# A decoder block with dilated attention and an RG-LRU: a third output tile and swapped PSUM banks in the attention stage, other engines for a few small operations

## The chip, the cores and the metric

The kernel runs on one core of a Trainium2 chip. The metric is the time of one execution on the device in microseconds (us), as the median of several runs. One further execution was recorded by the hardware profiler; all rows of the profile come from it.

Five engines work side by side, each through its own instructions in order: TensorE (PE; its weight loads are PEld), VectorE (DVE), ScalarE (ACT), GpSimd (POOL) and SyncE (SP, which here issues most of the DMAs). They wait for one another by semaphores. PSUM, into which TensorE writes, has eight banks of 128 x 512 float32. SBUF holds all other tiles.

## The reference, cut to what matters

```python
proj = x @ w_in + b_in                       # x: (1, 2048, 1024), w_in: 1024 x 9216
q, k, v, g_attn, u_lru, g_lru, gate_logits = split(proj)
# 3 head groups of 8 heads (64 wide): (window, dilation) = (128,1), (512,4), (2048,16)
for g in range(3):                           # rotary q and k, keys gathered by stride
    o_g, lse_g = dilated_band_attention(q[g], k[g], v[g], window, dilation)
attn = sum(softmax(lses) * outs) * silu(g_attn);          y_a = attn @ w_attn_proj
h = rg_lru(causal_conv(u_lru));              y_b = (h * silu(g_lru)) @ w_lru_proj
merged = sigmoid(gate_a) * y_a + sigmoid(gate_b) * y_b
out = layer_norm(2 ** 0.25 * x + merged @ w_out + b_out) * ln_gain + ln_bias
```

Everything is float32. Within `dilated_band_attention` each block of 128 queries meets at most 256 keys: scores, maximum, exponential with its sum, and the weighted sum of values.

## The kernel before, in words

The order of the instructions on each engine is written out by hand. Work that is to come a step later is put on a list (`later(lag, fn)`) and emitted by `run(late)` at the start of that step. Each matmul of the reference is made of three, from a high and a low part of either operand. There are three stages, each with pools of its own, which lie one over the other in SBUF and PSUM: a tile of a later stage waits for what still uses the earlier one's memory.

**First stage: the projection** (`product`, L622), up to 1443.8 us of the profile. It works through 72 passes of seven or eight products of 12 matmuls each, in four PSUM banks (tag `q`). VectorE and ScalarE take the results out (`total`, L568 and L227), and chains of small operations (`qk_chain`, `lru`, `mg_chain` and others) finish them and store them to DRAM. Results lie in 32 slots of SBUF of 2 KB per partition, numbers 0 to 31; `take` gives out the slot that has been free for longest, but for results `y` of the last pass it prefers those in the list `LATE`. The last gates `y` go through a tanh on ScalarE (L384) and are stored by ScalarE's DMA queue (L386).

**Second stage: attention**, up to the first `yb` matmul at 1654.6 us. There are 12 units, one for each pair of heads (two heads of one group), in the order of dilation 1, 16, 4, 1, 16, 4 and so on. A unit has four steps, so there are `NG` = 48 steps `i` and three more to run out; one step has four blocks `j` of 128 queries, with the two heads `h`. Tiles and their operations, where L is the line in the profile:

- `scores(i)`: TensorE writes the scores into four tiles `s` (L1005), one bank each.
- `peak(i, j, h)`: VectorE adds the mask and takes the maximum into `sta` (L1012), a small tile for each unit, 3 buffers; `expo(i, j, h)`: ScalarE takes the exponential, with its sum also into `sta` (L1020).
- `turn(i, w)`: TensorE transposes the weights of two blocks (`w` = 0: blocks 0 and 1) into two tiles `pt` (L1030). These and `o` share the tag `t`, four banks.
- `bring(i, w, k, eng)`: the copy of one such tile from PSUM into `ptb`, by ScalarE (L1043) or VectorE (L1045).
- `values(i)`: TensorE multiplies with the values into `o` (L1058); `leave(i)`: VectorE copies `o` into the unit's output tile `ot` (L1067, L1071 and L1069 for dilations 1, 16 and 4), 128 x 2048 float32, 2 buffers.
- SP stores `ot` to `o_scr` (L1073 for each step, L1075 for a whole unit of dilation 16) and, once for each unit, `sta` to `st_scr` (L1080, L1082; four DMAs in L1085). It also loads the next units' keys (L816, tile `B`), queries (L826, tile `A`) and values (tile `V`); GpSimd and others split the keys into high and low part (L809, L811).

In one step the engines get their work in this order:

```python
light = copied and (unit((i - 2) // 4)[0] == 2 or i % 3 == 1)
scores(i); leave(i - 3)
bring(i - 2, 1, 1, dve)
if light: bring(i - 2, 1, 0, dve)
expo(i - 1, 2, 1)
if copied and not light: bring(i - 2, 1, 0, act)
expo(i - 1, 3, 0); expo(i - 1, 3, 1); peak(i, 0, 0); expo(i, 0, 0); # peaks of blocks 0 and 1
turn(i - 1, 0); bring(i - 1, 0, 0, act); bring(i - 1, 0, 1, dve)
# exponentials of blocks 0 and 1; peaks of block 2; values(i - 2); turn(i - 1, 1); peaks of block 3
```

`light` says which engine makes the copy `bring(i - 2, 1, 0)`: VectorE in the steps after a unit of dilation 16 and in each third step, ScalarE in the others. `unit(u)[0]` is the group, 2 for dilation 16.

A pool gives a tag its memory when the tag is first used. So in PSUM the scores `s` got the four banks that the projection's `q` had, and the tag `t` got those of its tags `t` and `g`. In the third stage `y` (four banks) came first, then `ct` (one) and `z` (three).

**Third stage**: the projection of the RG-LRU branch (`yb_job`, L1310 to L1316), the combination of the attention groups, the projection of attention (`ya_job`, L1388 to L1394, the sum `me` on GpSimd), and for each 128 rows `tt` the output matmul and the LayerNorm (`out_job`, `z` in L1420 to L1422). LayerNorm there: VectorE adds the residual (L1433), takes the statistics (L1436, L1439) into a small tile `mv` (mean, variance, two more columns); ScalarE takes the square root of the variance plus `EPS` (L1440); VectorE centres the first half of the columns (`centre`, L1444), inverts the root (L1448), improves it by one Newton step in four operations on one column (L1450 to L1453), scales the first half (L1457), centres the second and scales it. Each half is stored by a DMA. The last rows (`tt` = 15, `last`) take the same path, with SP's queue for the first half and ScalarE's for the second.

## Time and profile before

| | |
|---|---|
| time, median of three runs | 2114.82 us (2113.8 to 2116.68) |
| the profiled execution's time | 2113.77 us |
| its span in the profile | 2112.0 us |
| busy PE, DVE, ACT, POOL | 2088.6, 1663.8, 1120.5, 491.9 us |
| granted TensorE clock, mean | 0.997 |
| DMA | 524.69 MB, mean 248 GB/s |

A row of a timeline gives the start in us from the beginning of the span, the duration, the engine, the line of the kernel, the operation, out<-in by the tiles' names, the shapes, and how often it stands there in a run; in brackets is the idle time of the engine ahead of it and what ended it. A row of waits names who waited for whom: us in total, times, the longest. A row of a window gives the stretch, its length, each engine's busy time in it with its instructions, the granted clock of TensorE (1.00 is full), the busy share of the DMA engines and GB/s. A row of DMA issues gives how many, the size and the median us from issue to landing. A row of a group of instructions gives its busy time and the mean ns of one, then the idle time ahead of it.

### The profile page before, as it was taken

The numbers are of one execution on the slowest core, as the hardware profiler recorded it, in microseconds if no ns is written. First come the engines' busy times: TensorE is split into PE (matmuls) and PEld (weight loads), VectorE is DVE, ScalarE is ACT, GpSimd is POOL, SyncE is SP. The second block draws the span as 40 slices with busy tenths as digits, with TensorE's granted clock in tenths as the row PEclk, the third lists the DMA queues.
The fourth block names the chain that finished last, engine by engine and source line by source line (L and its number), as shares of the span: only waits on it lengthen the run. The fifth ranks groups of instructions, "written<-read, shape, count | busy, mean of one in ns | idle before, by whom it ended". The sixth has DMA issues, their size and how long they took to land.

```text
span 2112.0 us, 35853 instructions
## 1 busy us (share of the span) xinstructions
PE 2088.6 (99%) x12016; PEld 1729.0 (82%) x12016; DVE 1663.8 (79%) x3193; ACT 1120.5 (53%) x2348; POOL 491.9 (23%) x465
## 2 busy tenths in 40 slices
PE   8999999999999999999999999999999999999998
PEld 7888888888888888887888888888989888888887
DVE  8987888888888867787787887877989645576667
ACT  6356456457356565656567666667999411221100
POOL 1111111111111002231232232222536444331120
PEclk9999999999999999999999999999999999999999
DMA  8987997997997976677788788879998788864432
GB/s 271 268 273 223 276 284 209 284 289 234 273 291 237 329 221 200 213 238 212 249 252 274 255 251 269 257 223 382 296 303 263 238 283 274 302 245 155 161 110 70
DMA packets 345832, 524.69 MB, mean 248 GB/s; under 512 B 124208, under 2 KB 153904, under 8 KB 341808
## 3 DMA queue, kind: packets, MB, share of 16 engines
q1 hardware_dynamic: 325760, 489.54, 71.5%
q0 software_dynamic: 12256, 19.42, 5.5%
q10 hardware_dynamic: 7632, 13.44, 1.7%
q8 instruction: 96, 1.57, 0.3%
q14 instruction: 88, 0.72, 0.1%
HBM read 317.14 MB, written 190.45 MB: 240 GB/s over the span
## 4 chain that ended last, share of the span: by engine, by line
PE 91%; ACT 6%; DVE 2%; DMA 1%; issue 0%; SPq 0%
PE q L622 66%; ACT p L1020 5%; PE yb L1310 3%; PE yb L1311 3%; PE z L1420 3%; PE z L1421 3%; PE z L1422 3%; PE yb L1312 3%; PE ya L1388 1%; PE ya L1389 1%; PE ya L1390 1%; PE g L492 1%; PE vtp L358 1%; ACT ptb L1043 1%; PE o L1058 1%; DVE p L1012 1%
## 5 line engine op out<-in xcount | busy, mean ns | idle before, releaser
L622 PE MATMUL q<-xT,hS 128*128 128x512 f32 x1680 | 521.1, 391 | 0.0
L622 PE MATMUL q<-xT,l 128*128 128x512 f32 x1120 | 436.0, 389 | 0.0
L622 PE MATMUL q<-xB,hA 128*128 128x512 f32 x1248 | 389.1, 393 | 5.6 <-ACT xB L215 5.6
L622 PEld LDWEIGHTS q<-xT,hS 128*128 128x128 f32 x1680 | 312.8, 188 | 69.0 <-issue 5.5
L622 PE MATMUL q<-xB,l 128*128 128x512 f32 x904 | 353.0, 390 | 0.0
L622 PEld LDWEIGHTS q<-xB,hA 128*128 128x128 f32 x1248 | 233.7, 189 | 57.0 <-ACT xB L215 5.6
L622 PEld LDWEIGHTS q<-xT,l 128*128 128x128 f32 x1120 | 210.3, 188 | 44.1
L622 PEld LDWEIGHTS q<-xB,l 128*128 128x128 f32 x904 | 170.2, 188 | 36.3 <-DVE l L227 0.5
L1020 ACT ACTIVATE p<-p,sta 128x256 f32<-128x256 f32 (+1 forms) x384 | 175.7, 511 | 5.0 <-DVE sta L1012 4.8
L245 POOL DMA_DIRECT2D wS<-in_w_in_dram x70 | 62.0, 965 | 492.6 <-DMA wS<-in_w_in_dram 137.5
L622 PE MATMUL q<-xB,hS 128*128 128x512 f32 x560 | 174.0, 392 | 0.0
L622 PE MATMUL q<-xT,hA 128*128 128x512 f32 x560 | 173.0, 390 | 0.0
L269 ACT ACTIVATE hA<-wA 128x512 fp32r<-128x512 f32 x218 | 134.9, 623 | 55.4 <-DMA wA<-in_w_in_dram 19.8
L269 ACT ACTIVATE hS<-S 128x512 fp32r<-128x512 f32 x175 | 109.0, 623 | 76.4 <-DVE S L227 48.8
L227 POOL TENSOR_TENSOR S<-S,wA 128x512 f32<-128x512 f32 x35 | 45.6, 1304 | 392.3 <-DVE S L227 218.2
L622 PEld LDWEIGHTS q<-xT,hA 128*128 128x128 f32 x560 | 104.7, 188 | 23.0 <-issue 1.5
L622 PEld LDWEIGHTS q<-xB,hS 128*128 128x128 f32 x560 | 104.0, 188 | 22.4 <-issue 1.5
L1012 DVE CUSTOM_DVE_ANT_0 p<-s,mask 128x256 f32<-128x256 f32 (+1 forms) x384 | 116.7, 363 | 1.3 <-PE s L1005 0.9
L1421 PE MATMUL z<-wo,mh 128*128 128x512 f32 (+1 forms) x264 | 101.0, 383 | 0.0
L1422 PE MATMUL z<-wo,ml 128*128 128x512 f32 (+1 forms) x264 | 101.0, 383 | 0.0
L1420 PE MATMUL z<-wo,mh 128*128 128x512 f32 (+1 forms) x264 | 101.0, 383 | 0.0
L1310 PE MATMUL yb<-h,wl 128*128 128x512 f32 x256 | 100.2, 392 | 0.0
(201 smaller groups left out, 4262.9 us busy)
## 6 DMA issues: line engine op xcount, KB each, us to landing
wA<-in_w_in_dram SPq DMA_DIRECT2D x253, 256.0 KB, 4.8
wl_scr<-l SPq DMA_DIRECT2D x105, 512.0 KB, 5.2
l<-wl_scr SPq DMA_DIRECT2D x105, 512.0 KB, 4.8
sw<-y SPq DMA_DIRECT2D x384, 64.0 KB, 3.3
wS<-in_w_in_dram SPq DMA_DIRECT2D x70, 256.0 KB, 4.8
wS<-in_w_in_dram POOLq DMA_DIRECT2D x70, 256.0 KB, 6.4
qh_scr<-hi SPq DMA_DIRECT2D x48, 256.0 KB, 5.6
v_scr<-vs SPq DMA_DIRECT2D x48, 256.0 KB, 4.8
```

Source lines behind the costliest of these rows:

```text
L227: eng.tensor_tensor(out=out, in0=in0, in1=in1, op=op)
L245: pool.dma_start(t, w_part(s, x), accum_op=ALU.add)
L269: act.activation(h, r, AF.Copy)
L622: pe.matmul(bank, w[:, ks], x[:, kk, xx], start=(first and i == 0), stop=(last and i == 11))
L1012: dve.tensor_tensor_reduce(out=st["p", i, j][:, h, lo:256], in0=st["s", i, j // 2][h][:, j % 2, lo:256], in1=mask[:, lo:256], scale=1.0, s ...
L1020: act.activation(p, p, AF.Exp, scale=-1.0, bias=s[:, h:h + 1], accum_out=s[:, 2 + h:3 + h])
L1310: pe.matmul(yb, WL[f][:, 0, k], xx[:, 0], start=(k == 0), stop=False)
L1311: pe.matmul(yb, WL[f][:, 0, k], xx[:, 1], start=False, stop=False)
L1312: pe.matmul(yb, WL[f][:, 1, k], xx[:, 0], start=False, stop=(k == 7))
L1420: pe.matmul(z, mh[:, k], w[:, 0, hs], start=(k == 0), stop=False)
L1421: pe.matmul(z, mh[:, k], w[:, 1, hs], start=False, stop=False)
L1422: pe.matmul(z, ml[:, k], w[:, 0, hs], start=False, stop=(k == 7))
```

## The change

1. **`LATE`** lists seven slots, 7 to 13, where it had five, 31, 7, 8, 9 and 30.
2. **PSUM banks.** In attention the tag `t` is used first, by a tile that nothing else uses, so `t` gets the first four banks and `s` the last four. In the third stage `ct` and `z` come first, so `y` gets the last four.
3. **`ot`** has 3 buffers. That takes 8 KB more per partition, and the tiles that follow in SBUF (`ptb`, then some of keys, queries and values) lie 8 KB higher.
4. **Copies.** In steps 47 and 48 `bring(i - 1, 0, 0)` is VectorE's, and step 48 is `light`, so that its `bring(i - 2, 1, 0)` is VectorE's too.
5. **LayerNorm of the last rows.** GpSimd fills a column of `mv` with -0.5, adds `EPS` to the variance and raises the sum to the power of -0.5; VectorE centres both halves and then scales both. The square root, the inverse and the Newton step are left out there.
6. **LayerNorm of the other rows.** The Newton step takes three operations on one column instead of four.

```diff
-    LATE = [31, 7, 8, 9, 30]
+    LATE = [7, 8, 9, 10, 11, 12, 13]
...
     aps = stB.enter_context(tc.tile_pool(name="aps", bufs=2, space=PSUM, reuse_waits="tile"))
+    aps.tile([P, 4, P], F32, tag="t", name="t", bufs=4)
...
-            ot[u] = at_p.tile([P, S], F32, tag="ot", name=f"ot{u}")
+            ot[u] = at_p.tile([P, S], F32, tag="ot", name=f"ot{u}", bufs=3)
...
-        light = copied and (unit((i - 2) // 4)[0] == 2 or i % 3 == 1)
+        light = copied and (unit((i - 2) // 4)[0] == 2 or i % 3 == 1 or i == NG)
...
-            bring(i - 1, 0, 0, act)
+            bring(i - 1, 0, 0, act if i < NG - 1 else dve)
...
     fp = ctx.enter_context(tc.tile_pool(name="fp", bufs=2, space=PSUM, reuse_waits="tile"))
+    fp.tile([P, 4, P], F32, tag="ct", name="ct", bufs=1)
+    fp.tile([P, CH], F32, tag="z", name="z", bufs=3)
...
-        act.activation(mv[:, 2:3], mv[:, 1:2], AF.Sqrt, bias=epst)
         halves = (slice(0, CH), slice(CH, D))
 
         def centre(hs):
             dve.scalar_tensor_tensor(out=x[:, hs], in0=x[:, hs], scalar=mv[:, 0:1], in1=vec[1][:, hs],
                                      op0=ALU.subtract, op1=ALU.mult)
 
-        centre(halves[0])
-        dve.reciprocal(out=mv[:, 2:3], in_=mv[:, 2:3])
-
-        dve.tensor_scalar(out=mv[:, 1:2], in0=mv[:, 1:2], scalar1=EPS, scalar2=-0.5, op0=ALU.add, op1=ALU.mult)
-        dve.tensor_tensor(out=mv[:, 3:4], in0=mv[:, 2:3], in1=mv[:, 2:3], op=ALU.mult)
-        dve.tensor_scalar(out=mv[:, 3:4], in0=mv[:, 3:4], scalar1=mv[:, 1:2], scalar2=1.5, op0=ALU.mult, op1=ALU.add)
-        dve.tensor_tensor(out=mv[:, 2:3], in0=mv[:, 2:3], in1=mv[:, 3:4], op=ALU.mult)
+        if last:
+            pool.memset(mv[:, 3:4], -0.5)
+            pool.tensor_tensor(out=mv[:, 2:3], in0=mv[:, 1:2], in1=epst, op=ALU.add)
+            pool.tensor_tensor(out=mv[:, 2:3], in0=mv[:, 2:3], in1=mv[:, 3:4], op=ALU.pow)
+            for hs in halves:
+                centre(hs)
+        else:
+            act.activation(mv[:, 2:3], mv[:, 1:2], AF.Sqrt, bias=epst)
+            centre(halves[0])
+            dve.reciprocal(out=mv[:, 2:3], in_=mv[:, 2:3])
+
+            dve.tensor_scalar(out=mv[:, 1:2], in0=mv[:, 1:2], scalar1=EPS, scalar2=-0.5, op0=ALU.add, op1=ALU.mult)
+            dve.scalar_tensor_tensor(out=mv[:, 3:4], in0=mv[:, 2:3], scalar=mv[:, 2:3], in1=mv[:, 1:2], op0=ALU.mult, op1=ALU.mult)
+            dve.tensor_scalar(out=mv[:, 2:3], in0=mv[:, 3:4], scalar1=1.5, scalar2=mv[:, 2:3], op0=ALU.add, op1=ALU.mult)
         for hs, eng in zip(halves, (sp, act) if last else (act, act)):
-            if hs.start:
+            if hs.start and not last:
                 centre(hs)
             dve.scalar_tensor_tensor(out=x[:, hs], in0=x[:, hs], scalar=mv[:, 2:3], in1=vec[2][:, hs],
                                      op0=ALU.mult, op1=ALU.add)
```

## The prediction

> **What bounds the kernel now.** I read the page first, then the waits of TensorE, the windows of 6 us, and the timelines at the four places where the diff touches something.

> ```profile
> PE 2088.6 (99%) x12016; PEld 1729.0 (82%) x12016; DVE 1663.8 (79%) x3193; ACT 1120.5 (53%) x2348; POOL 491.9 (23%) x465
> ```

> TensorE is busy for 2088.6 of 2112.0 us, and the diff removes none of its work. What can be won lies in TensorE's gaps, in its clock, and behind its last matmul.

> ```profile
> PE q L622 <- ACT xB L215: 5.6, 1, 5.6
> PE pt L1030 <- DVE ot L1071: 3.4, 1, 3.4
> PE o L1058 <- ACT ptb L1043: 1.6, 6, 0.4
> PE pt L1030 <- ACT ptb L1043: 1.6, 4, 0.6
> PE pt L1030 <- DVE ot L1069: 1.1, 1, 1.1
> PE s L1005 <- DVE y L227: 0.5, 1, 0.5
> PE s L1005 <- DVE sta L1012: 0.5, 2, 0.3
> PE o L1058 <- DVE ptb L1045: 0.4, 1, 0.4
> ```

> The waits of TensorE, whole (us in total, times, longest). The 5.6 us lie at the start, which the diff leaves alone; all other rows are of attention, none of the third stage. The single ones are a stall within attention (3.4), one at its end (1.1, and 0.4) and one at its beginning (0.5), and each has a part of the change. The windows show that the 3.4 us are not the whole of it (columns: us, busy PE, PEld, DVE, ACT, POOL, granted clock, DMA share, GB/s):

> ```profile
> 1572.00:1578.00 6.00, 2.57 (x46) 2.36 (x44) 1.88 (x10) 2.31 (x13) 0.00 (x0) 0.97 0.75 118
> 1578.00:1584.00 6.00, 6.00 (x64) 5.55 (x62) 5.03 (x33) 5.06 (x25) 1.05 (x2) 0.50 1.04 416
> ```

> After the gap the granted clock is 0.50 for the whole of the next window.

> **Part 1: third output tile (`ot`, bufs 2 to 3).** The same place of three successive groups of twelve attention steps, by the first score matmul of the second step of a dilation-16 unit:

> ```profile
> 1515.11 1.54 PE L1005 MATMUL s<-B,A 64*128 64x128 f32 x24
> 1564.90 1.53 PE L1005 MATMUL s<-B,A 64*128 64x128 f32 x24
> 1620.52 1.53 PE L1005 MATMUL s<-B,A 64*128 64x128 f32 x24
> ```

> Twelve steps take 1564.90 - 1515.11 = 49.79 us without the stall and 1620.52 - 1564.90 = 55.62 with it. The stall with its slow clock costs 55.62 - 49.79 = 5.8 us. Its cause:

> ```profile
> 1576.20 0.69 DVE L1071 COPY ot<-o 128x512 f32<-128x512 f32 x1 [4.12 <-issue]
> ...
> 1564.13 0.32 SPq L1073 DMA_DIRECT2D o_scr<-ot  x1
> ```

> ```profile
> o_scr<-ot SPq DMA_DIRECT2D x1, 256.0 KB, 12.0
> ```

> Unit 7 (step 31) takes the buffer of unit 5, whose last store was issued at 1564.13 and landed 12.0 us later, at 1576.1; VectorE's copy starts at 1576.20. With three buffers unit 7 takes that of unit 4, a whole unit (four steps, 49.79 / 3 = 16.6 us) further back. So the 5.8 us go, unless something else is late next. That I looked for: every tile that is reused near there. Keys, queries and values are early enough. The maxima's tile `sta` stays at three buffers, and its stores share the crowded queue:

> ```profile
> 1580.95 0.37 SPq L1080 DMA_DIRECT2D st_scr<-sta  x1
> ...
> 1543.46 0.28 DVE L1012 CUSTOM_DVE_ANT_0 p<-s,mask 128x128 f32<-128x128 f32 x1
> ```

> ```profile
> st_scr<-sta SPq DMA_DIRECT2D x1, 32.0 KB, 13.2
> ```

> Unit 9 (step 36) reuses unit 6's `sta`, whose store lands at 1580.95 + 13.2 = 1594.2, and nothing in the stall sets when that store is issued. Step 24 wrote its first maximum at 1543.46; 49.79 later is 1593.25. So VectorE will wait there for up to 1.0 us; today it comes 5.8 later and doesn't. ScalarE, which consumes the maxima, runs behind VectorE and covers some: I take +0.4, bounds 0 and +1.0 for this wait alone.

> **Part 2: swapped PSUM banks and `LATE`.** Score tiles now lie on the banks that the projection's transposes and gates used, not on those of its last products.

> ```profile
> 1443.77 0.32 PE L1005 MATMUL s<-B,A 64*128 64x128 f32 x1
> 1444.62 1.67 PE L1005 MATMUL s<-B,A 64*128 64x128 f32 x23 [0.53 <-DVE y L227]
> ...
> 1445.51 0.29 DVE L1012 CUSTOM_DVE_ANT_0 p<-s,mask 128x128 f32<-128x128 f32 x1 [0.94 <-PE s L1005]
> ...
> 1445.36 0.33 ACTq L386 DMA_DIRECT2D mg_scr<-y  x1
> 1445.84 0.40 ACT L1020 ACTIVATE p<-p,sta 128x128 f32<-128x128 f32 x1 [0.52 <-DVE sta L1012]
> ```

> TensorE no longer waits for VectorE's last result and starts its scores up to 0.85 earlier (the first score matmul starts at 1443.77 and the other 23 wait until 1444.62). VectorE follows. ScalarE doesn't: its last gate and that gate's store are issued until 1445.69, and its exponentials begin at 1445.84 now, 1445.70 then; from there the chain that ended last runs through ScalarE's exponentials. I take -0.1, bounds -0.85 and 0. In the third stage both pools keep their relation (its `y` banks are the scores' banks before and after), so there I count nothing: TensorE waits for nothing there today, as the list shows, and its four `y` banks are the cover; if that cover went, the price would be TensorE's wait for a free `y` bank. The slots in `LATE` and the 8 KB by which the tiles behind `ot` move change which loads wait for which stores; I count 0, as the first loads of the next stage are not awaited by TensorE.

> **Part 3: last copies on VectorE.** Three 128x512 copies (step 47's first, two of step 48) go from ScalarE to VectorE.

> ```profile
> 1647.68 0.69 DVE L1069 COPY ot<-o 128x512 f32<-128x512 f32 x1
> 1648.28 0.68 DVE L1045 COPY ptb<-pt 128x512 f32<-128x512 f32 x1
> ...
> 1648.84 0.63 ACT L1043 ACTIVATE ptb<-pt 128x512 f32<-128x512 f32 x1
> ...
> 1648.42 0.71 PE L1030 MATMUL pt<-ident,p 64*128 64x64 f32 x15 [1.08 <-DVE ot L1069]
> 1649.52 1.97 PE L1058 MATMUL o<-ptb,V 128*64 128x128 f32 x32 [0.39 <-ACT ptb L1043]
> ...
> 1653.58 1.09 PE L1058 MATMUL o<-ptb,V 128*64 128x128 f32 x16 [0.41 <-DVE ptb L1045]
> 1654.60 0.50 PE L1310 MATMUL yb<-h,wl 128*128 128x512 f32 x1
> ```

> VectorE's copies start 1648.28 - 1647.68 = 0.60 apart, and it has no idle time up to there. Step 47's copy now stands ahead of the four last maxima and of that copy of `ot` (1647.68), which frees the bank that TensorE's transposes wait for (1648.42): 0.60 later. Then come the copy of 1648.28 and behind it the one that ScalarE did at 1648.84: on VectorE it runs from 1649.48 to 1650.16 where ScalarE ended at 1649.47, so the values of 1649.52 start at some 1650.2. All behind it follows in TensorE's order: the next stage starts 0.6 later. That is a loss, by VectorE's being the later engine. The other bound: if ScalarE sets the pace, all three gaps can close, 1.08 + 0.39 + 0.41 = -1.9; the upper is three copies of 0.60, +1.8. I take +0.6.

> **Part 4: the factor of the last rows on GpSimd.**

> ```profile
> 2105.13 0.75 DVE L1444 SCALAR_TENSOR_TENSOR x<-x,mv,vec 128x512 f32<-128x512 f32 x1
> ...
> 2106.63 0.75 DVE L1457 SCALAR_TENSOR_TENSOR x<-x,mv,vec 128x512 f32<-128x512 f32 x1
> ...
> 2108.08 0.75 DVE L1457 SCALAR_TENSOR_TENSOR x<-x,mv,vec 128x512 f32<-128x512 f32 x1
> ```

> Behind the last matmul nothing hides anything. Today: centring, 0.67 later five single-column operations, at 2106.63 the first scaling, then centring, and at 2108.08 the last scaling. After: both centrings, then both scalings, 0.67 apart: the last would start at 2105.13 + 3 x 0.67 = 2107.14, a gain of 0.94, if the factor is there by 2106.47. GpSimd has 1.34 us for an addition and a power on one column; its fill can run early.

> ```profile
> L811 POOL TENSOR_TENSOR B<-B 128x512 fp32r<-128x512 f32 x44 | 56.5, 1285 | 3.5
> ...
> L1545 POOL MEMSET const-float32-0.0<- 128x1 f32 x1 | 0.1, 100 | 0.3 <-issue 0.3
> ...
> 2028.08 3.52 POOL L1394 TENSOR_TENSOR me<-gA,ybr 128x512 f32<-128x512 f32 x2 [11.39 <-DVE gA L1393]
> 2044.40 2.54 POOL L1394 TENSOR_TENSOR me<-gA,ybr 128x512 f32<-128x512 f32 x2 [12.80 <-DVE gA L1393]
> ```

> One column costs 0.1 (the fill), 512 columns of two inputs 1.29; no row shows a power. And two equal additions took 3.52 in one place and 2.54 in another, so 0.98 can be lost beside VectorE's work. If the two operations take T from 2105.1 on and are late, the last scaling starts at 2105.1 + T + 0.67, which is T - 2.31 against today's 2108.08. Addition and power at 0.1 each, with one such loss, are in time (-0.94); with two, T is 2.16 (-0.15); a power of 1.29 with two losses gives T = 3.35 (+1.0). I take -0.6, by the one-column row, with some loss; bounds -0.94 and +1.0.

> [...]

> For the other tiles the diff has one column operation fewer on VectorE, which waits for TensorE there: 0.

> **Sum.** -5.8 + 0.4 - 0.1 + 0.6 - 0.6 = -5.5 us. The profiled execution took 2113.77 (span 2112.0), so 2108.3; it was the fastest shown, 1.05 under the median. From the median: 2114.82 - 5.5 = 2109.3.

> **The rivals.** (a) The stall moves. The stores, keys and maxima between 1564 and 1594 land as one full queue allows, and only VectorE's wait for `ot` is taken out of it. If `sta` (or an operand I judged early) holds VectorE for 3 us in place of 1, some 2.5 of the 5.8 are left, and the total is -2.2: 2112.6. For it: `sta` is shown late by up to 1.0. Against: that row is the worst of those I found.

> (b) The slow clock doesn't come with every execution. It followed the one gap of 3.4 us; the gaps of 1.1 us and less in attention have no slow window behind them. If 3.4 is close to what it takes, a timed run may have the gap without the slow clock; part 1 then gains 3.4, and the total is 3.4 - 5.8 nearer to zero: -3.1, 2111.7. For it: it is the shortest gap with that effect in the trace. Against: the profiled run has the slow window and is the fastest shown. [...]

> (c) Slower: the power is computed in many steps on GpSimd, with no cover, between 2105.1 and the first scaling. Against the other parts' -4.9 the kernel is slower than before once T - 2.31 is over 4.9, T over 7.2 us, and by over 0.2% once T is over 11.4: 2119. For it: no row shows a power. Against: the dearest operation of GpSimd quoted here, on 512 times the columns, takes 1.29.

> (d) Part 3 wins and `sta` costs nothing: -1.9 for +0.6 and 0 for +0.4 make -8.4: 2106.4.

> **How the numbers follow.** What a measurement here can tell from no change is about 0.2%, 4.2 us: faster means under 2110.6. My forecast has 0.60 (own range 2107.6 to 2110.6), (d) 0.07, (a) 0.16, (b) 0.08, (c) 0.05, and 0.04 that the parts at their bad bounds leave within 0.2%. Faster: 0.60 + 0.07 = 0.67; same: 0.16 + 0.08 + 0.04 = 0.28; slower 0.05. The range runs from between (d) and the forecast, 2106.6, to just over (a), 2112.9; (c) and half of (d) are outside.

> **What would show it.** Right: no wait of TensorE for `ot` at step 31, no window at clock 0.50, twelve steps from unit 7 to unit 10 in some 50 us; a short VectorE wait ahead of step 36's first maximum; the first exponential 0.1 earlier against the last product; the first `yb` matmul some 0.6 later against the scores of step 47; the last scaling 0.4 to 0.9 nearer to the last matmul. Wrong: a wait of TensorE of over 2 us in attention, a new slow window, TensorE idle under `yb`, or GpSimd's power ending later than the second centring by over 1 us.

## The result, and the profile after

The changed kernel takes 2110.39 us (median of 19 runs, 2108.07 to 2116.29), the kernel before beside it 2114.87 (19 runs): the ratio is 0.9978, 95% interval 0.9971 to 0.9984, some 4.7 us less by the ratio (the two medians are 4.48 apart). The prediction was 2109.3. The profiled execution took 2109.35 us against the 2113.77 of before, 4.42 less, with a span of 2107.6. One execution in experiment 12 ran at a granted clock of 0.53 and took 8268 us; it does not enter the ratio there.

The page's engines, and the waits of TensorE in the changed kernel, whole (us in total, times, longest; lines have moved by one in attention and by two to nine behind it):

```profile
PE 2087.8 (99%) x12016; PEld 1727.2 (82%) x12016; DVE 1664.3 (79%) x3176; ACT 1119.5 (53%) x2344; POOL 493.5 (23%) x468
```

```profile
PE q L622 <- ACT xB L215: 5.7, 1, 5.7
PE pt L1031 <- ACT ptb L1044: 1.8, 5, 0.7
PE pt L1031 <- DVE ot L1070: 1.6, 1, 1.6
PE o L1059 <- ACT ptb L1044: 1.5, 6, 0.3
PE s L1006 <- DVE sta L1013: 0.6, 2, 0.3
PE o L1059 <- DVE ptb L1046: 0.4, 1, 0.4
PE pt L1031 <- ACT p L1021: 0.2, 1, 0.2
```

The wait of 3.4 for `ot` of L1071 is gone, and the 0.5 for `y`. The one at the end of attention (`ot`, L1069 before) has grown from 1.1 to 1.6. The two windows of the stall, which had clock 0.97 and 0.50:

```profile
1572.00:1578.00 6.00, 6.00 (x107) 5.43 (x105) 5.49 (x34) 6.00 (x32) 0.00 (x0) 1.00 0.70 134
1578.00:1584.00 6.00, 5.52 (x83) 4.70 (x84) 6.00 (x32) 6.00 (x28) 1.36 (x2) 1.00 1.04 410
```

TensorE is busy through the first, and the clock is full. To see where the time went, take the starts of seven instructions that both timelines have. In the changed kernel: the first exponentials of steps 0, 30, 42 and 46, the first `yb` matmul, the last `z` matmul (its end, 2100.44), and the two scalings of the last rows (together; the second starts at 2103.72 in the trace).

```profile
1445.75 0.40 ACT L1021 ACTIVATE p<-p,sta 128x128 f32<-128x128 f32 x1 [0.40 <-DVE sta L1013]
...
1570.45 0.57 ACT L1021 ACTIVATE p<-p,sta 128x128 f32<-128x128 f32 x1
...
1621.03 0.42 ACT L1021 ACTIVATE p<-p,sta 128x128 f32<-128x128 f32 x1
...
1635.27 0.56 ACT L1021 ACTIVATE p<-p,sta 128x256 f32<-128x256 f32 x1
...
1651.15 0.50 PE L1313 MATMUL yb<-h,wl 128*128 128x512 f32 x1
...
2100.16 0.28 PE L1425 MATMUL z<-wo,ml 128*128 128x256 f32 x1
...
2103.05 1.40 DVE L1466 SCALAR_TENSOR_TENSOR x<-x,mv,vec 128x512 f32<-128x512 f32 x2
```

The same instructions stand in the kernel before at 1445.84, 1570.49, 1626.26, 1640.52, 1654.60, 2103.88 (end) and 2108.08. The differences, by stretch:

| stretch (us) | before | after | change | forecast |
|---|---|---|---|---|
| last `q` matmul's end to first exponential (banks) | 2.00 | 1.89 | -0.11 | -0.1 |
| step 30 to step 42 (stall, then `sta`) | 55.77 | 50.58 | -5.19 | -5.8 + 0.4 |
| step 46 to first `yb` (copies) | 14.08 | 15.88 | +1.80 | +0.6 |
| first `yb` to last `z` (third stage) | 449.28 | 449.28 | 0 | 0 |
| last `z` to last scaling (LayerNorm) | 4.20 | 3.29 | -0.91 | -0.6 |

Together -4.41; the spans differ by 4.35. These five stretches are read in every trace below. The projection ahead of them isn't: its end lay between 1443.35 and 1445.60 in the fourteen traces of this case, and two kernels that do not differ in it (experiments 7 and 10) have both ends of that range; this scatter of 2 us is one reason why the times, with intervals of some 0.1% (2 us) to either side, separate the kernel before from the faster versions but hardly these from one another.

### The profile page after: what moved, and what is told of

Read it like the earlier page. It is cut to its first block, busy times and chain, and to the rows that moved or that the text cites. A ratio compares the mean times of both kernels' runs of the same rounds, so it can differ in the third digit from the quotient of the medians.

```text
span 2107.6 us, 35835 instructions
## 1 busy us (share of the span) xinstructions
PE 2087.8 (99%) x12016; PEld 1727.2 (82%) x12016; DVE 1664.3 (79%) x3176; ACT 1119.5 (53%) x2344; POOL 493.5 (23%) x468
## 5 line engine op out<-in xcount | busy, mean ns | idle before, releaser
L622 PE MATMUL q<-xT,hS 128*128 128x512 f32 x1680 | 521.1, 391 | 0.0
L622 PE MATMUL q<-xT,l 128*128 128x512 f32 x1120 | 436.0, 389 | 0.0
L622 PE MATMUL q<-xB,hA 128*128 128x512 f32 x1248 | 388.9, 393 | 5.7 <-ACT xB L215 5.7
L622 PEld LDWEIGHTS q<-xT,hS 128*128 128x128 f32 x1680 | 312.9, 188 | 68.9 <-issue 5.5
L622 PE MATMUL q<-xB,l 128*128 128x512 f32 x904 | 352.8, 390 | 0.1
L622 PEld LDWEIGHTS q<-xB,hA 128*128 128x128 f32 x1248 | 233.4, 188 | 57.8 <-ACT xB L215 5.7
L622 PEld LDWEIGHTS q<-xT,l 128*128 128x128 f32 x1120 | 210.2, 188 | 44.1
L622 PEld LDWEIGHTS q<-xB,l 128*128 128x128 f32 x904 | 170.1, 188 | 36.5 <-DVE l L227 1.0
L622 PE MATMUL q<-xB,hS 128*128 128x512 f32 x560 | 174.1, 392 | 0.0
L622 PE MATMUL q<-xT,hA 128*128 128x512 f32 x560 | 173.0, 390 | 0.0
L227 POOL TENSOR_TENSOR S<-S,wA 128x512 f32<-128x512 f32 x35 | 45.6, 1302 | 391.6 <-DVE S L227 229.1
L622 PEld LDWEIGHTS q<-xT,hA 128*128 128x128 f32 x560 | 104.7, 188 | 23.0 <-issue 1.5
L622 PEld LDWEIGHTS q<-xB,hS 128*128 128x128 f32 x560 | 104.0, 188 | 22.4 <-issue 1.5
L1021 ACT ACTIVATION_READ_ACCUMULATOR p<-p,sta 128x1 f32 x384 | 102.5, 267 | 0.0
## 6 DMA issues: line engine op xcount, KB each, us to landing
wA<-in_w_in_dram SPq DMA_DIRECT2D x253, 256.0 KB, 4.8
wS<-in_w_in_dram SPq DMA_DIRECT2D x70, 256.0 KB, 4.9
wS<-in_w_in_dram POOLq DMA_DIRECT2D x70, 256.0 KB, 6.3
qh_scr<-hi SPq DMA_DIRECT2D x48, 256.0 KB, 5.6
v_scr<-vs SPq DMA_DIRECT2D x48, 256.0 KB, 4.4
```

The source lines that it names most:

```text
L227: eng.tensor_tensor(out=out, in0=in0, in1=in1, op=op)
L622: pe.matmul(bank, w[:, ks], x[:, kk, xx], start=(first and i == 0), stop=(last and i == 11))
L1021: act.activation(p, p, AF.Exp, scale=-1.0, bias=s[:, h:h + 1], accum_out=s[:, 2 + h:3 + h])
```

## Experiments

**1. The third output tile alone.** The kernel before with one edit:

```diff
-            ot[u] = at_p.tile([P, S], F32, tag="ot", name=f"ot{u}")
+            ot[u] = at_p.tile([P, S], F32, tag="ot", name=f"ot{u}", bufs=3)
```

> The kernel before with a third output tile and nothing else. Theory A (each part of the change acts by itself, and its shift shows at its own place in the trace): the first exponential of step 31 comes 4.0 earlier than in the kernel before, that of step 37 5.2 earlier (5.5 for the stall, less 0.25 for the waits for the maxima's tile), the end of attention and everything behind it too: -5.2 us against the kernel before, no window of clock 0.50. Rival B (the parts lean on one another: the bank swap or the moved copies are needed for the stall to go, or the end of attention loses 1.8 by itself once it comes 5.2 earlier and meets other transfers): -3.4 or less.

Measured: 2107.81 against 2113.07 us, ratio 0.9977 (0.9968 to 0.9986). Step 30 to step 42 takes 49.71, the end of attention 14.28, the other stretches are those of the kernel before (2.00, 4.20); the clock stays full. So this one edit brings as much as the whole change, and theory A holds. It even passed steps 32 and 36 without the waits for `sta` that I had counted in.

**2. Without the three copies.** The changed kernel with two edits:

```diff
-        light = copied and (unit((i - 2) // 4)[0] == 2 or i % 3 == 1 or i == NG)
+        light = copied and (unit((i - 2) // 4)[0] == 2 or i % 3 == 1)
...
-            bring(i - 1, 0, 0, act if i < NG - 1 else dve)
+            bring(i - 1, 0, 0, act)
```

> The changed kernel with the three copies of steps 47 and 48 given back to ScalarE. Theory A (the copies make VectorE the later engine there): TensorE's first yb matmul comes 1.8 earlier than in the changed kernel, 5.2 earlier than in the kernel before, and the time is -6.2 us against the kernel before. Rival B (the end of attention is late for another reason, its place in memory or in the banks): first yb matmul as in the changed kernel within 0.3, -4.4 us.

Measured: 2107.71 against 2113.07, 0.9974 (0.9964 to 0.9984). The end of attention takes 14.06: the copies cost 1.8, as theory A has it. The first `yb` matmul came only 4.36 earlier than in the kernel before, for reasons that are not the copies: the projection ended 0.22 later, TensorE stood idle for 0.7 in step 19 with no releaser named (0.4 of it is left in the exponentials), and step 30 to step 42 took 50.91. That last one is a wait which the changed kernel's trace has too, but does not name. There, at step 32, and here at step 36:

```profile
1577.09 0.29 DVE L1013 CUSTOM_DVE_ANT_0 p<-s,mask 128x128 f32<-128x128 f32 x1 [0.51 <-ACT p L1021]
```

```profile
1595.08 0.29 DVE L1013 CUSTOM_DVE_ANT_0 p<-s,mask 128x128 f32<-128x128 f32 x1 [1.38 <-DMA st_scr<-sta]
```

The second is the wait of step 36 for the store of unit 6's maxima, 1.38 long, named. The first is put down to ScalarE, but the last of the four stores of unit 5's `sta` lands at 1576.93 in that trace, 0.16 ahead of the start.

**3. Four buffers for the maxima.** The changed kernel with `bufs=4` for `sta`.

> The changed kernel with four buffers for the maxima's tile sta in place of three. Theory A (the first maxima of steps 32 and 36 wait for the stores of the tiles of units 5 and 6, landed at 1576.93 and 1594.01): both waits of VectorE go (0.51 and 0.26 of idle time), the twelve steps from step 31 to step 43 take 49.75 in place of 50.58, -0.8 us against the changed kernel, -5.2 against the kernel before. Rival C (what is late there are the operands or ScalarE, as the profile names it): the twelve steps stay at 50.6, -4.4 us.

Measured: 2108.75 against 2113.07, 0.9974 (0.9966 to 0.9983). Step 31 to step 43 takes 49.71 in place of 50.58, and VectorE waits at neither step: theory A. But how much it wins depends on the execution. Of the seven traces with three `ot` and three `sta` and no delay put in, two took 50.58 and 50.91 from step 30 to step 42, the other five 49.71 to 49.73; the three with four `sta` all took 49.70 to 49.73. In the five without a wait the last stores of units 5 and 6 landed 0.7 to 2.7 us ahead of the first maxima of steps 32 and 36, which reuse their tiles; in the other two VectorE stood idle for 0.26 to 1.38 us ahead of such a maximum.

**4. Both.** Four buffers for `sta`, no tail copies.

> Both together: four buffers for sta, and the three copies back on ScalarE. Theory A: the two gains add, -0.8 and -1.8 against the changed kernel, -7.0 against the kernel before. Rivals B and C: -4.4, or the gain of one part alone.

Measured: 2107.07 against 2113.07, 0.9970 (0.9959 to 0.9980), some 6 us under the kernel before where 7.0 was expected. The trace has 49.70, 14.28 and 3.28 in the three stretches, its span is 2105.8. By its stretches it is 2.5 us under the changed kernel, level with experiment 5, where the store happened not to be late; by the times, the intervals of the two ratios overlap.

**5 and 6. Which of the copies.** The changed kernel, in both with the light copy of step 48 on ScalarE again; in 5 step 47's as well:

```diff
-            bring(i - 1, 0, 0, act if i < NG - 1 else dve)
+            bring(i - 1, 0, 0, act if i < NG else dve)
```

> The changed kernel with one of the three copies on VectorE: only step 48's first one (bring(47, 0, 0)); step 47's and the light one are ScalarE's again. The mark is the time from the first exponential of step 46 to the first yb matmul: 14.08 us in the kernel before, 15.88 with all three copies, 14.06 with none. Theory A (each copy adds its own 0.6 on VectorE, whichever it is): 14.7. Rival D (ScalarE's copies of step 48 come so late behind its last exponentials that VectorE makes this one for nothing, and step 47's or the light one carries the whole cost): 14.1.

> The changed kernel with two of the three copies on VectorE: step 47's and step 48's bring(i - 1, 0, 0); the light one is ScalarE's again. Same mark. Theory A (0.6 for each): 15.3. Rival D: 14.1 if the light copy carries it, 15.9 if step 47's does.

Measured, in one execution each: 14.25 with step 48's copy alone, 16.00 with step 47's beside it. Theory A, 0.6 for each copy, fails: step 47's copy carries it all, the other two nothing that stands out of the scatter (14.06 to 14.29 with neither step 47's copy nor the light one on VectorE, 15.74 to 16.20 with step 47's). Step 47's copy by itself was not run. The prices of the instructions can't explain 1.7 for a copy of 0.6. The windows behind the gap do; the changed kernel first, then experiment 4 (us, busy PE, PEld, DVE, ACT, POOL, clock, DMA share, GB/s):

```profile
1642.15:1643.79 1.64, 0.01 (x1) 0.00 (x1) 1.64 (x8) 1.64 (x9) 1.56 (x3) 1.00 0.93 175
1643.79:1644.60 0.81, 0.81 (x18) 0.74 (x20) 0.81 (x2) 0.49 (x2) 0.81 (x1) 1.00 0.33 37
1644.60:1648.00 3.40, 3.40 (x34) 3.07 (x34) 1.53 (x3) 0.00 (x0) 3.24 (x5) 0.50 0.60 113
```

```profile
1642.04:1643.12 1.08, 0.00 (x1) 0.00 (x1) 1.08 (x6) 1.08 (x7) 1.08 (x1) 1.00 1.04 149
1643.12:1644.00 0.88, 0.71 (x15) 0.57 (x15) 0.62 (x2) 0.88 (x5) 0.80 (x3) 1.00 0.44 21
1644.00:1647.40 3.40, 3.17 (x60) 2.94 (x62) 1.77 (x3) 1.64 (x6) 3.32 (x4) 1.00 0.61 96
```

With step 47's copy ahead of the last maxima, the gap of TensorE is 1.64 where it was 1.08, and behind it the clock is 0.50 for 3.40 us: 34 matmuls where 60 go through in the other kernel. The changed kernel has a slow stretch of its own, shorter than the one that it lost.

**7 and 8. A gap made on purpose.** The changed kernel, VectorE's copy of unit 7's first quarter made five times more, and seven times more (8 in place of the 6 shown):

```diff
-            dve.tensor_copy(t.rearrange("p (j r) -> p j r", r=16)[:, :, 4 * q:4 * q + 4], o.rearrange("p r j -> p j r"))
+            for _ in range(6 if i == 28 else 1):
+                dve.tensor_copy(t.rearrange("p (j r) -> p j r", r=16)[:, :, 4 * q:4 * q + 4], o.rearrange("p r j -> p j r"))
```

> The changed kernel with VectorE's copy of the first quarter of unit 7 into ot (step 31) made six times in place of once, five copies of 0.6 us more, so that VectorE is held there for 3.0 us and TensorE for some 2.2. Theory A with a clock that falls after the length of the gap (the gap of 3.4 us was followed by 6 us at clock 0.50, gaps of up to 1.6 were not): no window of clock 0.50, the first exponential of step 33 some 2.8 later than in the changed kernel, less what the waits for sta take today, +2.0 us against it, -2.4 against the kernel before. Rival E (any gap over 2 us is followed by the slow clock): +3.5 to +4.4 against the changed kernel, 0 to -1 against the kernel before.

> The same with seven copies more: VectorE is held for 4.2 us as by the store in the kernel before, TensorE for 3.4, with no store that is late. Theory A (the gap itself brings the slow clock, whatever caused it, in every execution): a window at clock 0.50, the first exponential of step 33 some 5.5 later than in the changed kernel, +4.7 us against it, 0 against the kernel before. Rival F (the slow clock goes with the crowded transfers of the kernel before, or comes only in some executions): +3.2 against the changed kernel, -1.2 against the kernel before, or times that fall into two groups 1.5 apart.

Measured: 2114.51 and 2116.96 against 2111.87, ratios 1.0014 (1.0004 to 1.0023) and 1.0021 (1.0011 to 1.0031). Copies into one place each wait for the one before (0.03 idle) and start 0.72 apart, not 0.60, so the gaps were longer than meant: 2.94 and 4.40 us. Experiment 7's gap and what follows, then experiment 8's slow stretch:

```profile
1572.90:1575.84 2.94, 0.00 (x1) 0.03 (x1) 2.84 (x5) 0.60 (x4) 0.00 (x0) 1.00 0.82 229
...
1576.80:1583.60 6.80, 6.80 (x76) 6.02 (x72) 5.42 (x34) 6.00 (x31) 1.94 (x3) 0.50 1.00 349
```

```profile
1577.50:1587.70 10.20, 9.01 (x91) 8.14 (x93) 8.13 (x43) 6.74 (x33) 4.75 (x6) 0.50 1.02 415
```

**9. The power beside an idle VectorE.** Experiment 4's kernel with a second fill, addition and power, on a scratch column, while VectorE waits for the last `z` product:

```diff
+                if last and n == 3:
+                    dm = cst.tile([P, 2], F32, tag="dm", name="dm", bufs=1)
+                    pool.memset(dm[:, 1:2], -0.5)
+                    pool.tensor_tensor(out=dm[:, 0:1], in0=st_[:, 2, 0:1], in1=epst, op=ALU.add)
+                    pool.tensor_tensor(out=dm[:, 0:1], in0=dm[:, 0:1], in1=dm[:, 1:2], op=ALU.pow)
```

> The kernel of the fourth run (four buffers for sta, no tail copies) with a second fill, addition and power of GpSimd on a scratch column, placed where VectorE waits for the last z product (2.0 us idle); the output does not use them. Theory G (GpSimd is not held up by VectorE's centring, an addition on one column costs 0.19 and a power 0.89 by themselves): both pairs show 0.19 and 0.89 within 0.05. Rival H (GpSimd and VectorE exclude one another, part of the 0.89 is a wait for the centring's end): the pair beside the idle VectorE is shorter, the power 0.5 or less. The last scaling stays 3.28 behind the end of the last z matmul by both.

Measured, GpSimd's rows and VectorE's centrings (L1451) and scalings (L1471):

```profile
2098.18 0.19 POOL L1444 TENSOR_TENSOR dm<-st,epst 128x1 f32<-128x1 f32 x1 [37.32 <-DVE st L1439]
2098.45 0.57 POOL L1445 TENSOR_TENSOR dm<-dm 128x1 f32<-128x1 f32 x1
...
2101.36 0.19 POOL L1456 TENSOR_TENSOR mv<-mv,epst 128x1 f32<-128x1 f32 x1 [2.28 <-DVE mv L1447]
2101.63 0.88 POOL L1457 TENSOR_TENSOR mv<-mv 128x1 f32<-128x1 f32 x1
```

```profile
2101.32 1.44 DVE L1451 SCALAR_TENSOR_TENSOR x<-x,mv,vec 128x512 f32<-128x512 f32 x2
2102.68 1.40 DVE L1471 SCALAR_TENSOR_TENSOR x<-x,mv,vec 128x512 f32<-128x512 f32 x2
```

Neither theory holds as written. The addition takes 0.19 in both places, and beside the centring it starts 0.04 after it; the power takes 0.57 alone and 0.88 beside the centrings, 0.31 more. The company is the likely cause, but the two powers also start from different values, and whether that has a part was not tried. VectorE loses nothing: its four instructions follow one another, and the last scaling stays 3.28 behind the last `z`. This is one execution, and its third stage takes 450.91 us up to the last `z`, 1.6 more than in the other traces: at 1861 and 1863 us TensorE waits 0.55 for `mh` and 0.79 for `ml`, the two parts of the sum `me`, over 230 us ahead of the added operations. Why is open.

**10. The old banks.** The changed kernel without the three lines that order the tags in PSUM.

> The changed kernel with the PSUM banks in the old order in attention and in the third stage. Theory A: the first exponential comes 2.00 us behind the end of the last q matmul, as in the kernel before (1.89 in the changed kernel), TensorE waits again 0.5 for VectorE's last y, and nothing else differs: the third stage from the first yb to the first z matmul takes 209.4 us as before (209.45 in both). Rival I (the swap was needed for the third stage, or moves other waits): the third stage is longer or shorter by over 0.2.

Measured, in one execution: 2.00 from the last `q` matmul to the first exponential, and TensorE's wait for `y` is back; first `yb` to first `z` 209.47. Theory A: the swap is worth 0.11, and nothing else that shows.

```profile
1446.38 1.67 PE L1005 MATMUL s<-B,A 64*128 64x128 f32 x23 [0.53 <-DVE y L227]
```

**11. The gap filled.** The changed kernel, its copies on VectorE, with matmuls that nobody reads in the gap:

```diff
+        if i == NG:
+            dz = aps.tile([P, 2, 256], F32, tag="s", name="dz", bufs=4)
+            QA, QB = units[11]
+            for _ in range(12):
+                pe.matmul(dz[:, 0, :], QA[0:64, 0, 0:P], QB[0:64, 0, 0:256], start=True, stop=True)
         if turns:
             turn(i - 1, 0)
```

> The changed kernel, its three copies on VectorE, with twelve matmuls more on TensorE in the gap of 1.64 us that follows step 47's scores (into a score bank that nobody reads afterwards; 0.11 us each). The copies of VectorE, which TensorE waits for there, stay as late as they are. Mark: first exponential of step 46 to first yb matmul, 15.88 in the changed kernel, 14.06 without the copies. Theory J (the copies make the gap 0.56 longer, and a gap of 1.64 is followed by one stretch of 3.4 us at clock 0.50 where one of 1.08 is not): no clock under 0.9 behind the gap, mark 14.6 to 14.8, -5.6 us against the kernel before. Rival K (the clock falls anyway, or the 1.8 are the copies themselves): mark 15.7 or more, -4.4.

Measured: 2108.74 against 2113.06, 0.9981 (0.9971 to 0.9990); the mark, the time from the first exponential of step 46 to the first `yb`, is 14.44.

```profile
1641.22 1.68 PE L1158 MATMUL dz<-B,A 64*128 64x256 f32 x12
1642.74 0.21 PE L1031 MATMUL pt<-ident,p 64*128 64x64 f32 x1
1643.15 0.71 PE L1031 MATMUL pt<-ident,p 64*128 64x64 f32 x15 [0.19 <-DVE ot L1070]
1643.79 1.97 PE L1059 MATMUL o<-ptb,V 128*64 128x128 f32 x32
```

```profile
1644.00:1647.40 3.40, 3.40 (x64) 2.95 (x60) 3.04 (x6) 0.00 (x0) 3.24 (x5) 1.00 0.83 217
```

The transposes still wait for VectorE (`ot`, 0.19 behind useless work), but the clock stays at 1.00 and the 32 value matmuls take 1.97 as they should. Twelve matmuls more on the engine that bounds the kernel make this stretch 1.44 us shorter. Of the 1.80 that the copies cost, 14.44 - 14.08 = 0.36 is their lateness and 15.88 - 14.44 = 1.44 the slow clock. That is the reading of one trace of each kernel: by the times this kernel is 4.0 to 4.3 us under the kernel before, where 5.6 was expected and the changed kernel has some 4.7, so the times do not show the gain.

**12. The kernel before, a second time.**

> The kernel before, unchanged, for a second trace of it. Theory A (the stall of step 31 belongs to the kernel, not to the one execution): TensorE waits 3 to 4 us for VectorE's ot in step 31, 6.8 us at clock 0.50 behind it, twelve steps from step 31's to step 43's predecessor 5 to 6 us longer than the twelve before; ratio 1.000 within its interval. Rival L (the store's landing differs by some us from one execution to the next, as the maxima's stores do): a wait under 2 or over 5 us, and another sum.

Measured: 2113.32 against 2113.06, ratio 1.000 (0.999 to 1.0009). Another pattern, nearly the same sum:

```profile
1574.32 0.69 DVE L1071 COPY ot<-o 128x512 f32<-128x512 f32 x1 [1.97 <-PE s L1005]
```

```profile
1593.49 0.69 DVE L1069 COPY ot<-o 128x512 f32<-128x512 f32 x1 [1.68 <-DMA o_scr<-ot]
```

```profile
1573.78:1575.07 1.29, 0.00 (x0) 0.00 (x1) 0.75 (x2) 0.60 (x4) 0.00 (x0) 1.00 0.50 156
1575.73:1582.55 6.82, 6.82 (x72) 6.16 (x68) 5.42 (x37) 5.63 (x27) 0.04 (x1) 0.50 0.91 274
1592.85:1594.24 1.39, 0.00 (x0) 0.00 (x0) 0.74 (x2) 1.00 (x5) 0.00 (x0) 1.00 0.73 112
1594.24:1601.00 6.76, 6.76 (x129) 6.41 (x131) 6.76 (x30) 5.84 (x22) 3.92 (x5) 1.00 0.98 382
```

Unit 5's store landed 1.9 us earlier, so step 31 waits 1.29 (with 6.8 us of slow clock all the same), and then step 35 waits for unit 6's store, which in the first trace the longer stall had hidden: there the copy of step 35 starts at 1593.67, here at 1593.49. Twelve steps take 55.27 here and 55.77 there. So rival L for the single waits, theory A for their sum: with two buffers the stores' landing times set the pace of two places, and a shorter wait at the first is collected at the second.

## Why the prediction was right, point by point

- **Third output tile: right, -5.8 forecast; experiment 1 alone -5.3 by the medians.** Nothing that I had judged early turned out late, but for the `sta` of step 32 in the next point. Rival (a) did not occur, though experiment 12 shows its mechanism in the kernel before. Rival (b) fails for the median: experiments 7 and 8 and both traces of before have the slow clock, and a kernel without the stall gains 5, not 3. It isn't excluded for every execution: in 19 of 74 further executions of before the granted clock was 0.999, as in all 26 of experiments 1, 2 and 4, whose traces have no slow stretch ahead of the last matmul. (If `sta` is what holds VectorE in rival (a), my -2.2 counted the +0.4 for it a second time; without it the sum is -2.6.)
- **The next late item, `sta`: right in kind.** I had named one wait, at step 36. The trace has two, at steps 32 and 36, and together they cost 50.58 - 49.71 = 0.87 against +0.4 forecast, in that execution; in five of the seven traces they cost nothing. The wait at step 32 is the longer one in the changed kernel, 0.51 against 0.26, and the trace of before could have shown it: the last of the four stores of unit 5's `sta` landed there at 1576.89, hidden by the stall.
- **Banks: right**, -0.11 against -0.1, and 0 in the third stage, with ScalarE's last gate and the issue of its store (until 1445.71) as the reason why only 0.1 of the 0.85 comes through. `LATE`, which I had at 0, was not tried by itself; no stretch shows it.
- **The tail's copies: the step that failed.** The direction was right, and so was the mechanism: VectorE is the later engine, and the gap of TensorE in front of step 47's transposes grew by 0.56 (1.08 to 1.64) where I had 0.60. What failed is "All behind it follows in TensorE's order: the next stage starts 0.6 later". I had the clock in the argument for the stall and not here, although this was the very place where the prediction made a gap longer. So one of my own signs of being wrong came true, a new slow window. The copies measured +1.80, of which 1.44 is the clock. The upper bound, three copies of 0.60, holds the number by accident: two of the three copies cost nothing.
- **The factor on GpSimd: a little better**, -0.91 against -0.6. The -0.6 stood for a T of some 1.7 (1.7 - 2.31), my estimate of the loss beside VectorE; no run shows such a T. In its place the trace has the power's end 1.21 behind the centring's start, inside the 1.34 that were free.

```profile
2101.69 1.44 DVE L1446 SCALAR_TENSOR_TENSOR x<-x,mv,vec 128x512 f32<-128x512 f32 x2
2101.74 0.19 POOL L1451 TENSOR_TENSOR mv<-mv,epst 128x1 f32<-128x1 f32 x1 [17.44 <-DVE mv L1442]
2102.01 0.89 POOL L1452 TENSOR_TENSOR mv<-mv 128x1 f32<-128x1 f32 x1
```

The addition starts 0.05 after the first centring and takes its 0.19, so in this trace the centring beside it does not hold it up; where experiment 9's 0.31 on the power comes from was not shown.

- **The sum: right by its largest term.** -5.5 forecast, -4.4 in the traces, some -4.7 in the times: 1.2 too little for the copies, 0.5 too little for `sta`, and the other way 0.3 for LayerNorm; the rest is rounding and the stall itself (-6.06 by steps 30 to 42, where the prediction's mark gave 5.83). The changed kernel keeps one part that loses (step 47's copy); without it, and with a fourth `sta`, experiment 4 has the lowest ratio here (0.9970), though its interval overlaps the others.

## What to carry to other kernels

Price a gap of TensorE by what follows it, too: in this kernel a gap that grew from 1.08 to 1.64 us cost 1.8, and filling it with useless matmuls took most of that back in the trace. When a wait on a buffer is removed, list the next late stores in the same queue; with two buffers the time won at one of them was given back at the next (a wait of 1.29 us where it had been 3.43, and twelve steps still took 55.27 for 55.77), with three it was kept (49.71 in experiment 1). And when a change has several parts, compare the traces stretch by stretch between the same instructions: the times said faster, and only the stretches said that one of the parts loses.

## What the hardware showed that I had not expected

The clock after a gap. In the fourteen traces every gap of TensorE of 1.1 us or less between its first matmuls and its last left the clock at 1.00 (seven of 1.08 or 1.09 at the end of attention, and all shorter ones); all six of 1.64 or 1.65 there were followed by one stretch of some 3.4 us at 0.50. In the middle of attention, 1.29, 2.94 and 3.43 were followed by 6.8 us and 4.40 by 10.2, but 1.39 (experiment 12, step 35) by none. The slow stretch begins 0.4 to 1.6 us after the matmuls have started again, and still within the gap of 4.40.

The stretches are all close to one, two or three times 3.4 us: 3.41 in the changed kernel, 6.83 and 6.82 in the two traces of the kernel before, 6.8 in experiment 7 and 10.2 in experiment 8. The length of the gap alone doesn't settle whether one follows, as 1.29 and 1.39 show. A second measure is how busy TensorE is around the gap. Here are stretches of 3.41 us, as long as the shortest slow one: the stretch that ends with the fall in the changed kernel, one with experiment 4's gap of 1.08, and two in experiment 12, one that has the gap of 1.29 and ends with the fall and one that has the gap of 1.39:

```profile
1641.20:1644.61 3.41, 1.77 (x40) 1.43 (x38) 3.41 (x12) 3.08 (x14) 3.25 (x4) 1.00 0.83 219
```

```profile
1640.38:1643.79 3.41, 2.33 (x50) 1.92 (x46) 3.28 (x13) 3.41 (x14) 3.33 (x4) 1.00 0.93 262
```

```profile
1572.32:1575.73 3.41, 2.12 (x39) 1.91 (x38) 1.44 (x6) 2.06 (x12) 0.00 (x0) 1.00 0.68 155
1592.80:1596.21 3.41, 2.02 (x40) 1.90 (x41) 2.71 (x11) 2.10 (x9) 0.00 (x0) 1.00 0.81 204
```

TensorE is busy for 52%, 68%, 62% and 59% of them; the clock fell after the first and the third. This share doesn't settle it either: why the 62% were followed by the slow clock and the 59% were not stays open. The share also depends on where such a stretch is laid around the gap, and what decides was not shown.
